# One written order for the experts' products on TensorE, and fifteen warm-up products instead of seven

## The chip, the cores and the metric

The kernel runs on one core of a Trainium2 chip. The metric is the device time of one execution in microseconds (us). The kernel before takes 1179.29 us, the median of 3 runs (1178.24 to 1180.68). Engines are named as in the profile: PE is TensorE's products, PEld its weight loads, DVE is VectorE, ACT is ScalarE, POOL is GpSimd, and SP is SyncE, which here issues most of the transfers.

## The reference: what is computed

Two layers of an encoder on 512 tokens of width 1024, all in float32. Each layer adds to `x` a mixer of two attention groups, then a cross-attention into 256 memory tokens, then a mixture of 16 experts; a last RMS norm follows. The change lies in the mixture:

```python
def expert_choice_moe(h, w_router, w_gate, w_up, w_down):
    cap = EC_CAPACITY_FACTOR * S // N_EXPERTS            # 64 tokens per expert
    affinity = jax.nn.softmax((h @ w_router).astype(jnp.float32), axis=-1)
    gate, idx = lax.top_k(jnp.swapaxes(affinity, 1, 2), cap)
    x_in = jax.vmap(lambda hb, ib: hb[ib])(h, idx)
    a = jnp.einsum('becd,edf->becf', x_in, w_gate)       # 1024 -> 512, per expert
    u = jnp.einsum('becd,edf->becf', x_in, w_up)
    y = jnp.einsum('becf,efd->becd', jax.nn.silu(a) * u, w_down)   # 512 -> 1024
    y = y * gate[..., None].astype(y.dtype)
    return jax.vmap(lambda ib, yb: jnp.zeros((S, D), yb.dtype).at[ib.reshape(-1)].add(yb.reshape(-1, D)))(idx, y)
```

## The kernel before

The two layers are written out one after the other (`for l in range(L)`). A layer's first part, the mixer and the memory attention, is not touched by the change. Then the router's affinities give each expert its 64 tokens: eight rounds of max, index and replace on DVE, two small products that place the indices (`placed`, L1012), and copies of them to `row`, `tok` and `gate` (L1014 to L1016). In layer 1 a helper `warm` (L980) puts products on PE whose result nobody reads: two behind each round, and `WARM_F` = 7 behind the index products (L1181), while the first tokens are gathered.

**Experts in pairs.** The 16 experts of a layer run as 8 pairs, p = 0 to 7. A pair's 128 tokens fill the 128 partitions: expert i of the pair has the 64 rows i\*64 to i\*64+63. For a pair the kernel does this:

- `fetch` (L1103, POOL) gathers the pair's 128 rows of 1024 values from HBM.
- `features_of(e, n)` (L1087) transposes one half of them on PE, four 128x128 transposes, and ACT (for the first pair DVE too) scales them into `xg`.
- `up_half(e, acc, w, kc)` (L1112) is half of the gate product (w = 0, into the bank `ag`) or of the up product (w = 1, into `au`): 8 products of 64 output rows by 512 columns, whose two experts alternate, i = 0, 1, 0, 1, and write different halves of the bank's partitions. In the trace each of these float32 products is two records.
- ACT takes the silu of `ag`, DVE multiplies it by `au` and the gate (L1214); `hid_t` (L1118) transposes the result and ACT copies it to `hT`.
- `down(e, n)` (L1131) is one half of the down product, 8 products of the same kind; ACT and DVE split the result into two parts `y` whose sum it is (L113, L114).
- `scatter(e, n)` (L1145) adds `y` to the tokens: for each of four blocks of 128 tokens two products, one per part, with a 0/1 matrix `sel` into a fresh bank, and DVE adds the bank to `x` (L1146). One such product is one record.

The pairs overlap by one: in pair p's turn PE does the first half of its gate product, the transposes of pair p-1's hidden values, half the features of p+1, the second gate half, pair p-1's down products, the first up half, the other features, pair p-1's two scatters, and the second up half.

**Weights.** The experts' weights are read from HBM in pieces of 512 KB ("loads" here), 24 per pair and 192 per layer, each holding two 512-column operands. SP issues them in the order of their use into some 40 slots, so that a load can start once the load 40 places before it has been used for the last time. Each load also waits for the load eight places before it, because the transfers of SP and ACT take eight completion semaphores (DMAHW0 to DMAHW7) in turn.

**What sets the order on an engine.** The kernel is written for a scheduler that puts instructions in an order of its own by its estimates of when they are ready; on the chip each engine then runs its instructions strictly in that order. `tc.issue_after(ins)` keeps what is written in its block behind `ins` on that engine. Before the change only a few such orders are given, none of them on the products of the experts, so the scheduler may put scatters between the products of an up half.

After the last pair's turn the rest is written out: `hid_t`, the second scatter of pair 6, `down(e, 0)`, the first half of `down(e, 1)`, `scatter(e, 0)`, the rest of `down(e, 1)`, `scatter(e, 1)`. In layer 1 `lnf`, the last norm's gains, is loaded by ACT (L1224) into a buffer that the gathered rows of pair 6 leave, and the final norm and four output transfers follow.

Of the kernel before, what the change touches and what calls it, by code (L numbers as in the profile page):

```python
# [16 lines left out]
P = 128  # L17
# [14 lines left out]
AFTER = 11  # L32
WARM_FROM = (8, 0)
WARM = 2
WARM_F = 7
XA = (2, 4)
MT = 6
MEM_EARLY = [0, 0, 2, 2]
# [20 lines left out]
def kernel(ctx: ExitStack, tc: tile.TileContext, a: dict, out: bass.AP):  # L59
    nc = tc.nc  # L60
# [17 lines left out]
    ident = const.tile([P, P], F32, name="ident")  # L78
# [126 lines left out]
    for l in range(L):  # L205
# [608 lines left out]
        for i in range(4):  # L814
            wh, wl = W.get()
            for h in range(4):
                for j in range(2):
                    k = 2 * i + j
# [258 lines left out]
        for p, e in enumerate(prs):  # L1077
            e.p = p

        def features_of(e, n):  # L1080

            if n == 0:
                e.xg = mp.tile([P, ND, P], F32, tag="xg", name=nm("xg"), bufs=3)
            pt = bank()
            for i in range(4):
                d = n * 4 + i
                nc.tensor.transpose(pt[:, i * P:(i + 1) * P], e.rows[:, d * P:(d + 1) * P], ident)  # L1087
            for i in range(4):
                d = n * 4 + i
                if e.p == 0 and i % 2:  # L1090
                    nc.vector.tensor_scalar(e.xg[:, d, :], pt[:, i * P:(i + 1) * P], gain(l, G_FFN, d), None, op0=ALU.mult)
                else:
                    nc.scalar.activation(e.xg[:, d, :], pt[:, i * P:(i + 1) * P], AF.Copy, scale=gain(l, G_FFN, d))  # L1093
# [12 lines left out]
        def up_half(e, acc, w, kc):  # L1106
            for j in range(4):
                k = kc * 4 + j
                if j % 2 == 0:
                    ch = [chunk(2 * e.p + i, w * 4 + k // 2) for i in range(2)]  # L1110
                for i in range(2):
                    nc.tensor.matmul(acc[i * 64:i * 64 + 64, :], e.xg[:, k, i * 64:i * 64 + 64],  # L1112
                                     ch[i][j % 2], start=k == 0, stop=k == 7)

        def hid_t(e):
            pH = bank()
            for f in range(4):
                nc.tensor.transpose(pH[:, f * P:(f + 1) * P], e.hid[:, f * P:(f + 1) * P], ident)  # L1118
            e.y = []
            e.hT = mp.tile([P, 4, P], F32, tag="sg", name=nm("hT"), bufs=1)  # L1120
            nc.scalar.copy(e.hT, pH.rearrange("p (f s) -> p f s", f=4))  # L1121

        def down(e, n, parts=(0, 1)):
            if parts[0] == 0:
                e.py = bank()
            for c in parts:
                ch = [chunk(2 * e.p + i, 8 + 2 * n + c) for i in range(2)]
                for j in range(2):
                    f = 2 * c + j
                    for i in range(2):  # L1130
                        nc.tensor.matmul(e.py[i * 64:i * 64 + 64, :], e.hT[:, f, i * 64:i * 64 + 64], ch[i][j],  # L1131
                                         start=f == 0, stop=f == 3)
            if parts[-1] == 1:
                t = mp.tile([P, 2, 512], F32R, tag="y", name=nm("y"), bufs=2)
                e.last = split(t[:, 0, :], t[:, 1, :], e.py)
                e.y.append((t[:, 0, :], t[:, 1, :]))

        def scatter(e, n):
            last = l == L - 1 and e.p == NE // 2 - 1
            for b in range(NB):  # L1140
# [1 line left out]
                o = bank()  # L1142
                sl = e.sel[:, b * P:(b + 1) * P]
                for i in range(2):
                    nc.tensor.matmul(o, sl, e.y[n][i], start=i == 0, stop=i == 1)  # L1145
                nc.vector.tensor_tensor(out=x[:, b, ns], in0=o, in1=x[:, b, ns], op=ALU.add)  # L1146
                if last and n == 0:
                    if b == 0:
# [37 lines left out]
        for e in prs:  # L1186
# [13 lines left out]
            if not end:  # L1200
                features_of(prs[e.p + 1], 1)
                if e.p + 2 < NE // 2:
                    fetch(prs[e.p + 2])
            if prev is not None and not end:
                for n in range(2):
                    scatter(prev, n)
            if not end:
                selection(e)
            up_half(e, au, 1, 1)
            if end:  # L1210
                scatter(prev, 0)
            sg = mp.tile([P, FF], F32, tag="sg", name=nm("sg"), bufs=1)
# [98 lines left out]
```

## Time and profile before

| | |
|---|---|
| median of 3 runs | 1179.29 us |
| the profiled execution | 1181.12 us |
| its span, first to last instruction | 1179.3 us |
| PE, busy and share of the span | 1141.4 us, 97% |
| DVE, ACT, POOL busy | 598.4, 489.2, 201.0 us |
| loads of the experts' weights | 384 of 512 KB |
| the experts of layer 0, first transpose to last scatter | 371.5 to 604.4 us |
| the experts of layer 1 | 937.1 to 1168.4 us |

The profiled execution is 1.8 us above the median; 1.8 us of its time lie outside its span. The span's times are counted from the first instruction. A busy PE is not PE at its peak: a row's records overlap, and what a stretch costs is read from the starts of the rows. "PEclk" is the granted share of TensorE's clock of 2.4 GHz. The DMA share is that of the core's 16 transfer engines; one at work all the time shows as 1.03 here.

### The profile page before, as it was taken

What the parts mean: (1) busy time and instruction counts of PE and PEld (TensorE: products, weight loads), DVE (VectorE), ACT (ScalarE), POOL (GpSimd) and SP (SyncE); (2) the same over time, 40 slices, a digit from 0 to 9 for tenths busy, and PEclk for the clock granted to TensorE, in tenths of its full rate; (3) what the DMA queues carried; (4) which work ended last, traced back from release to release, by engine and by line L of the source; (5) the groups of instructions that cost most, each with busy time, mean ns of one, the idle gap of its engine ahead of it and who ended that gap; (6) DMA issues with size and microseconds to landing.
All of it is one profiled execution on the core that took longest, in us unless ns stands there. A gap on an engine that the chain in (4) does not pass through costs nothing.

```text
span 1179.3 us, 16319 instructions
## 1 busy us (share of the span) xinstructions
PE 1141.4 (97%) x5842; PEld 721.4 (61%) x5842; DVE 598.4 (51%) x1354; ACT 489.2 (41%) x1116; POOL 201.0 (17%) x250
## 2 busy tenths in 40 slices
PE   7999999999999999999999999999999899999995
PEld 7977777788674343333369777777877433433332
DVE  4888967554652132222167888774565402322224
ACT  5378857464642111111043697573454221111103
POOL 2633323100011000000026323231000200000002
PEclk9999999999999999999999999999999799999998
DMA  6410111277168999999924200013833799997993
GB/s 196 134 63 10 36 37 36 72 279 293 54 231 329 411 410 410 410 409 409 358 73 134 85 1 21 16 55 114 308 114 110 300 386 410 409 411 295 410 409 156
DMA packets 78625, 259.67 MB, mean 220 GB/s; under 512 B 8528, under 2 KB 18640, under 8 KB 78544
## 3 DMA queue, kind: packets, MB, share of 16 engines
q1 hardware_dynamic: 74528, 245.41, 54.7%
q0 software_dynamic: 3584, 12.58, 2.8%
q8 instruction: 46, 0.75, 0.3%
q10 hardware_dynamic: 432, 0.63, 0.2%
q14 instruction: 35, 0.29, 0.1%
HBM read 252.30 MB, written 6.29 MB: 219 GB/s over the span
## 4 chain that ended last, share of the span: by engine, by line
PE 87%; DVE 5%; ACT 3%; issue 2%; DMA 2%; POOL 0%; SPq 0%; POOLq 0%; DVEq 0%; ACTq 0%
PE ps L1112 19%; PE ps L144 11%; PE ps L145 10%; PE ps L146 10%; PE ps L1131 10%; PE ps L1145 6%; PE ps L407 5%; PE ps L393 4%; PE ps L488 2%; DVE smm L181 2%; PE ps L1087 1%; DMA xrows<-xn 1%; PE ps L846 1%; PE ps L805 1%; PE ps L858 1%
## 5 line engine op out<-in xcount | busy, mean ns | idle before, releaser
L1112 PE MATMUL ps<-ew,xg 128*64 128x512 f32 x1024 | 260.5, 602 | 0.2 <-ACT xg L1093 0.2
L1112 PEld LDWEIGHTS ps<-ew,xg 128*64 128x64 f32 x1024 | 75.0, 137 | 142.4 <-issue 131.1
L114 DVE TENSOR_TENSOR y<-ps,y 128x512 fp32r<-128x512 f32 x32 | 21.9, 690 | 204.3 <-ACT y L113 204.3
L1131 PE MATMUL ps<-ew,hT 128*64 128x512 f32 x512 | 117.0, 593 | 0.0
L1146 DVE TENSOR_TENSOR x<-ps,x 128x512 f32<-128x512 f32 x128 | 81.0, 683 | 57.0 <-PE ps L1145 56.9
L181 DVE TENSOR_REDUCE smm<-ps 128x1 f32<-128x512 f32 (+1 forms) x144 | 97.5, 681 | 18.4 <-PE ps L488 7.7
L114 DVE TENSOR_TENSOR wlo<-raw,whi 128x1024 fp32r<-128x1024 f32 (+2 forms) x68 | 77.5, 1142 | 50.4 <-ACT whi L113 48.5
L187 ACT ACTIVATE P<-ps,smm 128x512 f32<-128x512 f32 x128 | 88.7, 696 | 27.7 <-DVE smm L181 22.0
L196 POOL TENSOR_TENSOR P<-P,smr 128x512 f32<-128x512 f32 x64 | 70.3, 1099 | 155.9 <-DVE smr L194 125.4
L113 ACT CAST whi<-raw 128x1024 fp32r<-128x1024 f32 (+2 forms) x68 | 65.8, 969 | 61.4 <-PE ps L145 32.4
L1131 PEld LDWEIGHTS ps<-ew,hT 128*64 128x64 f32 x512 | 37.3, 137 | 73.0 <-issue 72.2
L1121 ACT COPY hT<-ps 128x512 f32<-128x512 f32 x16 | 9.4, 586 | 173.9 <-PE ps L1118 173.9
L113 ACT CAST y<-ps 128x512 fp32r<-128x512 f32 x32 | 18.5, 586 | 147.9 <-PE ps L1131 139.0
L393 PE MATMUL ps<-ident,P 128*128 128x128 f32 x512 | 76.9, 274 | 2.8 <-POOL P L196 0.9
L393 PEld LDWEIGHTS ps<-ident,P 128*128 128x128 f32 x512 | 62.6, 141 | 22.8 <-issue 4.1
L1145 PE MATMUL ps<-y,sel 128*128 128x512 f32 x256 | 71.8, 412 | 2.1 <-ACT y L113 2.1
L144 PE MATMUL ps<-whi,hTh 128*128 128x384 f32 (+2 forms) x208 | 72.8, 350 | 0.3 <-ACT whi L113 0.3
L145 PE MATMUL ps<-whi,hTl 128*128 128x384 f32 (+2 forms) x208 | 72.2, 347 | 0.0
L146 PE MATMUL ps<-wlo,hTh 128*128 128x384 f32 (+2 forms) x208 | 72.1, 348 | 0.0
L1145 PEld LDWEIGHTS ps<-y,sel 128*128 128x128 f32 x256 | 44.5, 188 | 38.4 <-issue 17.8
L396 ACT COPY PT<-ps 128x512 f32<-128x512 f32 x96 | 55.9, 588 | 26.0 <-PE ps L393 25.7
L1103 POOL DMA_INDIRECT rows<-xrows,row x16 | 15.2, 953 | 245.2 <-PE ps L1145 152.6
(227 smaller groups left out, 2101.4 us busy)
## 6 DMA issues: line engine op xcount, KB each, us to landing
ew<-moe SPq DMA_DIRECT2D x384, 512.0 KB, 10.2
raw<-w_o SPq DMA_DIRECT2D x16, 512.0 KB, 3.7
raw<-w_mem_q SPq DMA_DIRECT2D x8, 512.0 KB, 4.6
raw<-w_mem_o SPq DMA_DIRECT2D x8, 512.0 KB, 3.9
xrows<-xn POOLq DMA_DIRECT2D x16, 256.0 KB, 7.5
raw<-w_in_c SPq DMA_DIRECT2D x8, 416.0 KB, 3.6
raw<-w_in_a SPq DMA_DIRECT2D x8, 384.0 KB, 5.8
raw<-w_in_b SPq DMA_DIRECT2D x8, 384.0 KB, 3.5
```

What stands on the lines that cost most here:

```text
L113: i = nc.scalar.copy(dst_hi, src)
L114: nc.vector.tensor_tensor(out=dst_lo, in0=src, in1=dst_hi.bitcast(F32), op=ALU.subtract)
L144: nc.tensor.matmul(o, lh, rh, start=start, stop=False)
L145: nc.tensor.matmul(o, ll, rh, start=False, stop=False)
L146: nc.tensor.matmul(o, lh, rl, start=False, stop=stop)
L181: nc.vector.tensor_reduce(out=m, in_=s.rearrange("p (g n) -> p g n", g=groups), axis=AX.X, op=ALU.max, negate=True)
L187: nc.scalar.activation(p[:, g * n:(g + 1) * n], s[:, g * n:(g + 1) * n], AF.Exp, bias=m[:, g:g + 1], scale=1.0 if scale is None else scale ...
L393: nc.tensor.transpose(pt[:, tb * P:(tb + 1) * P], u.p[:, tb * P:(tb + 1) * P], ident)
L1112: nc.tensor.matmul(acc[i * 64:i * 64 + 64, :], e.xg[:, k, i * 64:i * 64 + 64], ch[i][j % 2], start=k == 0, stop=k == 7)
L1131: nc.tensor.matmul(e.py[i * 64:i * 64 + 64, :], e.hT[:, f, i * 64:i * 64 + 64], ch[i][j], start=f == 0, stop=f == 3)
L1145: nc.tensor.matmul(o, sl, e.y[n][i], start=i == 0, stop=i == 1)
L1146: nc.vector.tensor_tensor(out=x[:, b, ns], in0=o, in1=x[:, b, ns], op=ALU.add)
```

## The change

All products, transposes and scatters of the experts go through one chain: each is issued behind the one before it in the order in which the kernel is written, beginning behind `placed`. Pair 0's scatters, which come in the turn of pair 1, are written behind pair 1's second up half instead of ahead of it. `WARM_F` goes from 7 to 15.

```diff
-WARM_F = 7
+WARM_F = 15
...
+        turn = [placed]
+
+        def in_turn(*args, **kw):
+
+            with tc.issue_after(turn[0].ins):
+                turn[0] = nc.tensor.matmul(*args, **kw)
+
         def features_of(e, n):
...
-                nc.tensor.transpose(pt[:, i * P:(i + 1) * P], e.rows[:, d * P:(d + 1) * P], ident)
+                with tc.issue_after(turn[0].ins):
+                    turn[0] = nc.tensor.transpose(pt[:, i * P:(i + 1) * P], e.rows[:, d * P:(d + 1) * P], ident)
...
-                    nc.tensor.matmul(acc[i * 64:i * 64 + 64, :], e.xg[:, k, i * 64:i * 64 + 64],
-                                     ch[i][j % 2], start=k == 0, stop=k == 7)
+                    in_turn(acc[i * 64:i * 64 + 64, :], e.xg[:, k, i * 64:i * 64 + 64],
+                            ch[i][j % 2], start=k == 0, stop=k == 7)
...
-                    nc.tensor.matmul(o, sl, e.y[n][i], start=i == 0, stop=i == 1)
+                    in_turn(o, sl, e.y[n][i], start=i == 0, stop=i == 1)
...
-            if prev is not None and not end:
+
+            if prev is not None and not end and e.p > 1:
                 for n in range(2):
                     scatter(prev, n)
             if not end:
                 selection(e)
             up_half(e, au, 1, 1)
+            if e.p == 1:
+                for n in range(2):
+                    scatter(prev, n)
```

The transposes of `hid_t` and the products of `down` are changed in the same way. How the built programs differ is shown below at three places; numbers behind a name are buffers.

**PE, layer 1, the turn of pair 5**, from the first up half to the second: L1112 (now L1085) is `up_half`, L1087 (now L1095) `features_of`, L1145 (now L1085 as well, since the helper issues it) `scatter` of pair 4. Before:

```order
L1112 MATMUL ps_9858<-ew_9859,xg_9621 64x512
L1087 MATMUL ps_9875<-ident,rows_9713 128x128 x4
L1145 MATMUL ps_9886<-y_9835,sel_9747 128x512 x2
L1112 MATMUL ps_9858<-ew_9861,xg_9621 64x512
L1112 MATMUL ps_9858<-ew_9859,xg_9621 64x512
L1112 MATMUL ps_9858<-ew_9861,xg_9621 64x512
L1145 MATMUL ps_9890<-y_9835,sel_9747 128x512 x2
L1145 MATMUL ps_9894<-y_9835,sel_9747 128x512
L1112 MATMUL ps_9858<-ew_9867,xg_9621 64x512
L1145 MATMUL ps_9894<-y_9835,sel_9747 128x512
```

and with the change:

```order
L1085 MATMUL ps_9866<-ew_9875,xg_9629 64x512
L1085 MATMUL ps_9866<-ew_9877,xg_9629 64x512
L1085 MATMUL ps_9866<-ew_9875,xg_9629 64x512
L1085 MATMUL ps_9866<-ew_9877,xg_9629 64x512
L1095 MATMUL ps_9883<-ident,rows_9721 128x128 x4
L1085 MATMUL ps_9894<-y_9843,sel_9755 128x512 x2
L1085 MATMUL ps_9898<-y_9843,sel_9755 128x512 x2
L1085 MATMUL ps_9902<-y_9843,sel_9755 128x512 x2
```

Before, the first up half's eight products stand in runs of one, three, one and three, with scatter products between; now they stand in one run, and the sixteen scatter products in another. Before, the turns of pairs 3 to 7 in layer 0 and of pairs 4 to 7 in layer 1 have such a place, and in layer 0's turn of pair 1 the scatters split an up half into runs of five and three; now no turn has one, and those of pairs 2 to 6 have the form shown second.

**SP, layer 1, the loads around the last norm's gains**, with the semaphores that each waits for. Before:

```order
L1054 DMA ew_9869<-moe 128x1024 [waits DMAHW3_49,PE_49]
L1054 DMA ew_9920<-moe 128x1024 [waits DMAHW5_49,PE_49]
L1054 DMA ew_9922<-moe 128x1024 [waits DMAHW6_49,PE_49]
L1054 DMA ew_9928<-moe 128x1024 [waits DMAHW7_49,PE_49]
...
L1054 DMA ew_9948<-moe 128x1024 [waits DMAHW3_49,PE_49]
L1054 DMA ew_9950<-moe 128x1024 [waits DMAHW4_49,PE_49]
```

and with the change:

```order
L1054 DMA ew_9928<-moe 128x1024 [waits DMAHW4_49,PE_49]
L1054 DMA ew_9930<-moe 128x1024 [waits DMAHW5_49,PE_49]
L1054 DMA ew_9936<-moe 128x1024 [waits DMAHW6_49,PE_49]
L1054 DMA ew_9938<-moe 128x1024 [waits DMAHW0_49,PE_49]
...
L1054 DMA ew_9983<-moe 128x1024 [waits DMAHW6_49,PE_49]
L1054 DMA ew_9989<-moe 128x1024 [waits DMAHW7_49,PE_49]
```

The semaphore that SP's loads leave out there belongs to the load of `lnf` that ACT issues (in both programs ACT's load stands behind the first scaling of pair 6's second features). Before it is DMAHW4, and the load into `ew_9950` is the first that waits for it; now it is DMAHW7, and three more loads stand ahead of the first that waits, the one into `ew_9989`.

**ACT, the first work of layer 1's mixer**: L150 is a sum of squares, L116 the first part of a transposed block of `x`, L113 the first part of a weight. Before:

```order
L116 ACTIVATE hTh_5403<-ps_5412,gains 128x512
L150 ACTIVATE junk_5524,nss_5467<-x 128x512
L116 ACTIVATE hTh_5419<-ps_5421,gains 128x512
L113 CAST whi_5392<-raw_5391 128x2x384
L116 ACTIVATE hTh_5419<-ps_5428,gains 128x512
L113 CAST whi_5398<-raw_5397 128x2x384
```

and with the change:

```order
L116 ACTIVATE hTh_5403<-ps_5412,gains 128x512
L116 ACTIVATE hTh_5419<-ps_5421,gains 128x512
L116 ACTIVATE hTh_5419<-ps_5428,gains 128x512
L116 ACTIVATE hTh_5435<-ps_5437,gains 128x512
L113 CAST whi_5392<-raw_5391 128x2x384
L113 CAST whi_5398<-raw_5397 128x2x384
```

The first weight's cast, for which the first product of the layer waits, stands behind two more activations and ahead of one sum of squares that it followed before.

## Rows read from the trace of the kernel before

**Rows 1.** The page's part 1: busy us, share of the span and instructions of each engine.

```profile
PE 1141.4 (97%) x5842; PEld 721.4 (61%) x5842; DVE 598.4 (51%) x1354; ACT 489.2 (41%) x1116; POOL 201.0 (17%) x250
```

**Rows 2.** Windows: stretch, us, busy us (x instructions) by engine, PEclk, DMA share, GB/s.

```profile
471.62:501.86 30.24, 30.16 (x124) 11.11 (x125) 7.68 (x12) 4.54 (x12) 0.94 (x1) 1.00 1.03 410
1013.16:1039.34 26.18, 26.18 (x127) 10.89 (x125) 7.40 (x12) 4.45 (x12) 0.94 (x1) 1.00 1.03 410
1065.85:1096.09 30.24, 30.16 (x124) 11.12 (x125) 7.68 (x12) 4.53 (x12) 0.00 (x0) 1.00 0.78 298
```

**Rows 3.** PE in order of time (start, us, records at x): turn of pair 3, then 5.

```profile
1028.48 3.91 PE L1145 MATMUL ps<-y,sel 128*128 128x512 f32 x16
1032.32 7.09 PE L1112 MATMUL ps<-ew,xg 128*64 128x512 f32 x32
...
1082.96 1.93 PE L1112 MATMUL ps<-ew,xg 128*64 128x512 f32 x6
```

**Rows 4.** SP's loads for pair 7's up product: layer 0, then layer 1.

```profile
L1054 SPq DMA_DIRECT2D ew<-moe x8: 327/327/328, 557.1 to 566.1; - x8
...
DMA to landing us min/median/max: 10.2/10.2/10.2
...
L1054 SPq DMA_DIRECT2D ew<-moe x8: 328/328/328, 1128.5 to 1137.4; - x8
...
DMA to landing us min/median/max: 10.2/10.2/10.5
```

**Rows 5.** PE and DVE in order of time: layer 0 from pair 7's up product on, then layer 1.

```profile
576.27 0.59 PE L1112 MATMUL ps<-ew,xg 128*64 128x512 f32 x1
...
582.10 5.36 PE L1112 MATMUL ps<-ew,xg 128*64 128x512 f32 x22
...
599.56 1.94 PE L1131 MATMUL ps<-ew,hT 128*64 128x512 f32 x8
...
602.21 0.69 DVE L114 TENSOR_TENSOR y<-ps,y 128x512 fp32r<-128x512 f32 x1 [1.73 <-ACT y L113]
...
1140.25 0.59 PE L1112 MATMUL ps<-ew,xg 128*64 128x512 f32 x1
...
1146.09 5.36 PE L1112 MATMUL ps<-ew,xg 128*64 128x512 f32 x22
```

**Rows 6.** ACT in order of time, first work of layer 1.

```profile
606.17 0.63 ACT L150 ACTIVATE junk<-x 128x512 bf16<-128x512 f32 x1
...
606.78 0.68 ACT L116 ACTIVATE hTh<-ps,gains 128x512 fp32r<-128x512 f32 x1
```

**Rows 7.** PE in order of time: the first pair of layer 0, then of layer 1.

```profile
371.51 1.04 PE L1087 MATMUL ps<-ident,rows 128*128 128x128 f32 x8
372.74 3.65 PE L1112 MATMUL ps<-ew,xg 128*64 128x512 f32 x16 [0.20 <-ACT xg L1093]
...
929.59 3.29 PE L984 MATMUL ps<-x 128*128 128x256 f32 x14
937.14 1.97 PE L1087 MATMUL ps<-ident,rows 128*128 128x128 f32 x8 [4.26 <-DMA rows<-xrows,row]
939.04 5.56 PE L1112 MATMUL ps<-ew,xg 128*64 128x512 f32 x16
```

**Rows 8.** SP's loads' waits (us, times, longest); the issue of `lnf`, its landing.

```profile
SPq L1054 <- PE ps L1112: 38.8, 33, 22.7
...
SPq L1054 <- DMA lnf<-lnf: 14.8, 1, 14.8
...
L1224 ACTq DMA_DIRECT2D lnf<-lnf x1: 334/334/334, 1082.8 to 1082.8; - x1
...
DMA to landing us min/median/max: 3.4/3.4/3.4
```

**Rows 9.** PE early in layer 1's mixer, and the window behind it.

```profile
669.74 1.14 PE L488 MATMUL ps<-kk,qs 128*128 128x512 f32 x2 [1.29 <-DVE qs L114]
...
670.00:673.30 3.30, 3.30 (x14) 2.04 (x15) 3.21 (x14) 3.07 (x6) 1.31 (x2) 0.50 0.00 0
```

More of the change, by code (lines that the diff above doesn't have):

```diff
@@ L1117, in hid_t @@
             for f in range(4):
-                nc.tensor.transpose(pH[:, f * P:(f + 1) * P], e.hid[:, f * P:(f + 1) * P], ident)
+                with tc.issue_after(turn[0].ins):
+                    turn[0] = nc.tensor.transpose(pH[:, f * P:(f + 1) * P], e.hid[:, f * P:(f + 1) * P], ident)
             e.y = []
@@ L1130, in down @@
                     for i in range(2):
-                        nc.tensor.matmul(e.py[i * 64:i * 64 + 64, :], e.hT[:, f, i * 64:i * 64 + 64], ch[i][j],
-                                         start=f == 0, stop=f == 3)
+                        in_turn(e.py[i * 64:i * 64 + 64, :], e.hT[:, f, i * 64:i * 64 + 64], ch[i][j],
+                                start=f == 0, stop=f == 3)
             if parts[-1] == 1:
```

## The prediction

> **What bounds the kernel now.** I read the page's part 1 first: PE is busy for 97% of the span, every other engine for 61% or less [rows 1]. Next come windows of one turn each, where the reader should compare the length with the DMA column [rows 2]. A turn of layer 1 whose products stand unbroken takes 26.18 us, a turn with scatters between the products of an up half 30.24 us, at the same granted clock, 1.00, and with the same products. PE in order of time shows why [rows 3]: an unbroken up half costs 7.09 / 32 = 0.22 us a record, while a run of three products (six records) costs 1.93 us where 1.33 would be due; each break leaves a half-bank product without its partner and costs about half a us. A broken turn loses 4.06 us to that.
>
> The transfers are the second bound, and a near one. In layer 0's broken turn they run at 410 GB/s with a share of 1.03, so they are never idle. SP issues eight loads in 9.0 us, one per 1.28 us, and each lands 10.2 us later, so eight are in flight [rows 4]. A turn's 24 loads need 30.7 us: PE at 30.24 us a turn already eats slowly into the lead of the loads, and at 26.18 us would run into them. That lead is the number on which this prediction rests. In layer 0 the first load of pair 7's up product lands at 557.1 + 10.2 = 567.3 and is first used at 576.27: 8.9 us. In layer 1 it lands at 1128.5 + 10.2 = 1138.7 and is used at 1140.25: 1.5 us [rows 4, 5]. Layer 1 has less because its stream starts late and is stopped once; both are seen in SP's waits, below.
>
> **The change, part by part.** *Breaks on PE.* The order rows show no break left. Layer 0 has three full pieces of 4.06 us (12.2), some 3.4 in the half turn ahead of them and 4.2 in the last turn, estimates by the same half us a break: 19.8 us of PE time. Layer 1 has two full pieces: 8.1 + 3.4 + 4.2 = 15.7. If PE alone set the end, that would be the gain. But PE then arrives at weights that have not landed, so I work out each layer's end from its last up load instead.
>
> *Layer 0.* Transfers are saturated, so PE's new order cannot bring the loads forward: the last up load of pair 7 still lands at 566.1 + 10.2 = 576.3. Six records that need it follow (1.35 us), so the up product ends at 577.65; in the kernel before it ended at 582.10 + 5.36 = 587.46 [rows 5]. That is 9.8 us earlier. Behind it stand, before and now, the last transposes, scatters and the down product. By PE's prices this tail is now 1.95 (eight scatters) + 0.5 (transposes) + 1.95 + 5.3 (24 down records) + 1.95 + 1.76 = 13.4 us, to 591.06. The tail before took 14.04 us, to 599.56 + 1.94 = 601.50. So the down product ends 10.4 us earlier. Its weights land behind the up loads, eight more at 1.28 us: 586.5, ahead of their last use at 589.3, so they do not bind.
>
> Two small terms go against it. The last scatter takes the two parts of `y` alternately now, and the second part is ready only behind DVE's 0.69 us [rows 5], where four first parts filled that time: +0.65. At the start of layer 1 the first weight's cast, for which PE waits, stands behind two more activations of 0.68 us and ahead of one sum of squares of 0.63 that it followed [rows 6]: +0.6, to nothing at best and 1.3 at worst; I take the difference. Layer 0: -10.4 + 0.65 + 0.6 = **-9.2 us**. Pair 0's scatters move behind the other up half of pair 1; they are the same products, and a delay there (about 0.65 us of PE) is hidden by the later wait for loads.
>
> *Layer 1, warm-ups.* Seven products took 3.29 us in 14 records and PE then idled 4.26 us until the rows landed. The first pair's transposes cost 1.97 us where layer 0's cost 1.04, and its first product 5.56 instead of 3.65 [rows 7]: half clock. Fifteen products are 30 records, 7.05 us at that price, and end at 936.6, 0.5 us ahead of the landing at 937.14, so they delay nothing by themselves, and the first block becomes 0.93 + 1.91 less 0.2 = 2.6 us shorter. If the clock stays low anyway this is 0; if the products overrun, they cost at most a us. Since the loads there wait for slots that PE frees (the longest wait is 22.7 us [rows 8]), the stream shifts with PE: I take -2.3.
>
> *Layer 1, the stop at `lnf`.* One load of SP waited 14.8 us for the load of `lnf`, issued by ACT at 1082.8 and landed 3.4 us later, at 1086.2 [rows 8]. The turn around it ran at 298 GB/s instead of 410: 30.24 x (1 - 298 / 410) = 8.3 us of stream lost, so a stop costs its length less 6.5 us, what was in flight. Now PE reaches the place that lets ACT issue `lnf` 6.0 us earlier (2.6 from the warm clock, 3.4 from the breaks ahead of it), so it lands at 1080.2; and three more loads go out first (the order rows: `ew_9989` instead of `ew_9950`), so the stop begins 3.8 us later in the stream, less the stream's own shift of 2.3. The stop shrinks to 14.8 - 6.0 - 1.5 = 7.3 us or a little more and costs about 1.1 us: -7.2. Bounds: whole stop left, 0; none left, -8.3.
>
> So layer 1's last up load lands 2.3 + 7.2 = 9.5 us earlier: 1137.4 + 10.5 - 9.5 = 1138.4. The up product ends at 1139.75 instead of 1146.09 + 5.36 = 1151.45 [rows 4, 5], 11.7 earlier; the same shorter tail gives 0.65, and the last scatter's first block is ready for DVE 0.25 earlier: **-12.5 us**, below what PE could gain by itself there (15.7 + 2.6 = 18.3).
>
> **Sum.** -9.2 - 12.5 = -21.7: the profiled execution's 1181.12 becomes 1159.4; it stood 1.8 above the median, so I predict **1158 us**. Less than 2.4 us (0.2%) could not be told from no change by a measurement of this kernel; faster means under 1176.9.
>
> **The rivals.** *The clock falls in the load-paced stretch (slower).* PE would work 1.76 us (eight records) and wait 0.8 in every 2.56 us (two loads) over pair 6's second half turn, pair 7 and the tail, some 46 us of PE work a layer. A gap of 1.29 us early in layer 1's mixer is followed by a window at a granted 0.50 [rows 9], 1.2 GHz, and at that level the transposes cost 1.9 times as much [rows 7]. If all of the stretch ran so, each layer would take 41 us more, of which up to 9.4 fill waits: +32 a layer, about 1222 us. Against it: one gap, and one wait of 4.26 us, stand behind those falls, with other engines' chains in between; here PE keeps two thirds. It is slower than before only if about half of the stretch is at half clock: 0.04. Milder swings or a stop at `lnf` left whole cost 7 to 18 us and end at 1165 to 1176, part of it inside my range; above it: 0.07.
>
> The Trainium skill, "TensorE: Matmul & The Clock Gate", section "A second HAM failure mode: psum-queue depth-cycling", tells of a kernel whose many micro-idles between groups of products made the clock swing between its two levels, at a loss of throughput. By that rule this change, which swaps slow but steady products for quick ones with waits, gives back its gain, and the sum would be the 1222 us above, or part of the way there. The trace of the kernel before shows such a fall in one place and none in the broken turns.
>
> *The loads do not bind.* If SP's loads ran on earlier than I think, PE's own time would decide: -19.8 - 18.3 = -38, about 1143 us. The share of 1.03 through layer 0 speaks against it: 0.04.
>
> *Nothing changes.* If the breaks only filled time that PE would have spent waiting for loads, the end stays near 1179. Layer 1's lead of 1.5 us speaks for it, layer 0's 8.9 us against; it also needs the stop to stay whole: 0.05. That the change does not do what it says is ruled out by the order rows.
>
> **How the numbers follow.** Forecast 0.80, clock or stop in a milder form 0.07, loads not binding 0.04, no change 0.05, clock falls for good 0.04. Faster: 0.80 + 0.07 + 0.04 = 0.91; same 0.05; slower 0.04. The range takes the bounds of the unknown prices: low, the stop gone (-1.1), the cast free (-0.6) and the down weights alone at the end of each layer (-2.4 a layer, what PE's tail exceeds them), 1151; high, the stop whole (+7.2) and the clock giving back about 1.4 a layer, 1168.
>
> **What the next profile would show.** Turns of pairs 2 to 5 at 26.2 us in both layers, with runs of 16 and 32 records at 0.22 us; PE's waits on landed weights, almost none before, at 7 to 9 us a layer in the turns of pairs 6 and 7; the transfers at 410 GB/s to the end; layer 0's experts ending at about 594 instead of 604.4; SP's wait on `lnf` near 7 us instead of 14.8; a granted clock of 1.00 at 937 and the first product at 3.65 us. Wrong would be: a clock below 1.00 in the last turns (first rival), an up product of pair 7 that ends well before 577.65 (loads not binding), or a stop at `lnf` as long as before.

## The result and the profile after

The changed kernel takes **1161.89 us**, the median of 4 runs (1161.59 to 1162.22), against 1179.21 us of the kernel before beside it: a ratio of 0.9853, 95% interval 0.9839 to 0.9866. That is 17.3 us faster; 1158 us was forecast, within 1151 to 1168. The profiled execution took 1162.13 us, its span is 1160.3 us. Run again later beside other kernels, it took 1162.75 us, ratio 0.9855 (0.9832 to 0.9878).

Part 1 of the page of the changed kernel, which answers to [rows 1]:

```profile
PE 1118.9 (96%) x5858; PEld 721.5 (62%) x5858; DVE 596.1 (51%) x1354; ACT 489.1 (42%) x1116; POOL 200.9 (17%) x250
```

PE's share fell by one per cent only: a row of PE reaches to its modelled end, so a wait of 0.8 us between two groups of products shows as 0.2 us of idleness. The waits are better read from the length of a turn. Windows of the changed kernel, in the columns of [rows 2]: three turns of layer 0 (from one pair's second features to the next pair's; the third ends with pair 7's up product), then the same three of layer 1:

```profile
484.12:510.30 26.18, 26.18 (x127) 10.93 (x125) 7.40 (x12) 4.44 (x12) 0.94 (x1) 1.00 1.03 409
510.30:540.66 30.36, 29.53 (x126) 11.49 (x124) 7.41 (x12) 4.44 (x12) 0.00 (x0) 1.00 1.03 409
540.66:576.47 35.81, 34.38 (x138) 12.65 (x137) 7.41 (x12) 3.40 (x8) 0.00 (x0) 1.00 1.03 409
...
1042.26:1068.43 26.17, 26.17 (x126) 10.89 (x124) 7.41 (x12) 4.44 (x12) 0.94 (x1) 1.00 1.03 410
1068.43:1097.08 28.65, 28.24 (x127) 11.42 (x125) 7.41 (x12) 4.44 (x12) 0.00 (x0) 1.00 0.91 355
1097.08:1133.05 35.97, 34.50 (x138) 12.60 (x137) 7.41 (x12) 3.40 (x8) 0.00 (x0) 1.00 1.03 409
```

Unbroken turns take 26.18 us now in both layers, until PE reaches weights that have not landed: in the turns that end at 540.66 and at 1097.08 and in those behind them PE waits for landings. The granted clock is 1.00 in all six windows. One window has transfers below their rate (355 GB/s): the stop at `lnf`, which is still there.

PE in order of time in the changed kernel: the end of layer 0's experts, the first work of layer 1, then the first and last products of layer 1's experts (L1085 issues all three kinds of product; the tiles tell them apart):

```profile
370.33 1.04 PE L1095 MATMUL ps<-ident,rows 128*128 128x128 f32 x8
...
559.25 2.36 PE L1085 MATMUL ps<-ew,hT 128*64 128x512 f32 x8 [0.21 <-DMA ew<-moe]
...
572.05 2.35 PE L1085 MATMUL ps<-ew,xg 128*64 128x512 f32 x8 [0.20 <-DMA ew<-moe]
574.61 1.93 PE L1085 MATMUL ps<-ew,xg 128*64 128x512 f32 x6 [0.21 <-DMA ew<-moe]
576.47 2.12 PE L1085 MATMUL ps<-y,sel 128*128 128x512 f32 x8
...
588.15 1.94 PE L1085 MATMUL ps<-ew,hT 128*64 128x512 f32 x8
590.83 0.49 PE L1085 MATMUL ps<-y,sel 128*128 128x512 f32 x1 [0.74 <-ACT y L113]
591.55 1.89 PE L1085 MATMUL ps<-y,sel 128*128 128x512 f32 x7 [0.23 <-DVE y L114]
...
597.86 0.44 PE L144 MATMUL ps<-whi,hTh 128*128 128x384 f32 x1 [0.93 <-ACT whi L113]
...
918.52 6.74 PE L984 MATMUL ps<-x 128*128 128x256 f32 x30
927.20 1.09 PE L1095 MATMUL ps<-ident,rows 128*128 128x128 f32 x8 [1.94 <-DMA rows<-xrows,row]
928.32 3.65 PE L1085 MATMUL ps<-ew,xg 128*64 128x512 f32 x16
931.90 0.66 PE L1095 MATMUL ps<-ident,rows 128*128 128x128 f32 x4
...
1131.19 1.93 PE L1085 MATMUL ps<-ew,xg 128*64 128x512 f32 x6 [0.22 <-DMA ew<-moe]
...
1144.74 1.94 PE L1085 MATMUL ps<-ew,hT 128*64 128x512 f32 x8
```

Groups of eight records start 2.56 us apart there (572.05, 574.61): two loads, as forecast. The warm-ups end before the rows land, and the first 16 records take 3.65 us. Two rows of the kernel before that were not shown, for the same places:

```profile
608.24 0.44 PE L144 MATMUL ps<-whi,hTh 128*128 128x384 f32 x1 [0.34 <-ACT whi L113]
...
1163.56 1.94 PE L1131 MATMUL ps<-ew,hT 128*64 128x512 f32 x8
```

With [rows 5, 7] the span divides so (us; the end of a row is its start and its length):

| from the end of the line above to | before | after | difference | forecast |
|---|---|---|---|---|
| first transpose of layer 0's experts | 371.51 | 370.33 | -1.18 | 0 |
| end of its last down product | 229.99 | 219.76 | -10.23 | -10.4 |
| first product of layer 1 | 6.74 | 7.77 | +1.03 | +1.25 |
| first transpose of layer 1's experts | 328.90 | 329.34 | +0.44 | 0 |
| end of its last down product | 228.36 | 219.48 | **-8.88** | -12.3 |
| end of the span | 13.80 | 13.62 | -0.18 | -0.25 |

The first line is not the change's: up to there the work is the same, and over the executions profiled here that place came between 369.25 and 372.45.

### The profile page after: what moved, and what is told of

It reads as the page before. It is cut to its first block, busy times and chain, and to the rows that moved or that the text cites. A ratio compares the mean times of both kernels' runs of the same rounds, so it can differ in the third digit from the quotient of the medians.

```text
span 1160.3 us, 16352 instructions
## 1 busy us (share of the span) xinstructions
PE 1118.9 (96%) x5858; PEld 721.5 (62%) x5858; DVE 596.1 (51%) x1354; ACT 489.1 (42%) x1116; POOL 200.9 (17%) x250
## 4 chain that ended last, share of the span: by engine, by line
PE 75%; DMA 15%; DVE 5%; ACT 3%; issue 1%; POOL 1%; SPq 0%; DVEq 0%; ACTq 0%; POOLq 0%
PE ps L1085 24%; DMA ew<-moe 12%; PE ps L144 11%; PE ps L145 10%; PE ps L146 10%; PE ps L407 5%; PE ps L393 4%; DVE smm L181 2%; PE ps L488 1%; DMA xrows<-xn 1%; PE ps L846 1%; PE ps L805 1%; PE ps L858 1%; PE ps L1095 1%; PE ps L250 1%
## 5 line engine op out<-in xcount | busy, mean ns | idle before, releaser
L1085 PE MATMUL ps<-ew,xg 128*64 128x512 f32 x1024 | 239.5, 597 | 2.7 <-DMA ew<-moe 2.5
L1085 PEld LDWEIGHTS ps<-ew,xg 128*64 128x64 f32 x1024 | 71.8, 136 | 144.2 <-issue 119.8
L1085 PE MATMUL ps<-ew,hT 128*64 128x512 f32 x512 | 121.0, 596 | 1.7 <-DMA ew<-moe 1.7
L1155 DVE TENSOR_TENSOR x<-ps,x 128x512 f32<-128x512 f32 x128 | 78.3, 684 | 37.7 <-PE ps L1085 37.7
L113 ACT CAST whi<-raw 128x1024 fp32r<-128x1024 f32 (+2 forms) x68 | 65.6, 969 | 61.7 <-PE ps L145 32.8
L1085 PEld LDWEIGHTS ps<-ew,hT 128*64 128x64 f32 x512 | 38.3, 137 | 80.0 <-issue 65.4
L113 ACT CAST y<-ps 128x512 fp32r<-128x512 f32 x32 | 18.5, 586 | 138.8 <-PE ps L1085 138.8
L1085 PE MATMUL ps<-y,sel 128*128 128x512 f32 x256 | 64.6, 400 | 3.0 <-ACT y L113 2.1
L1101 ACT ACTIVATE xg<-ps,gains 128x128 f32<-128x128 f32 x120 | 34.7, 371 | 62.0 <-PE ps L1095 61.7
L1085 PEld LDWEIGHTS ps<-y,sel 128*128 128x128 f32 x256 | 46.5, 188 | 19.6 <-ACT y L113 5.6
```

Source lines behind the costliest of these rows:

```text
L113: i = nc.scalar.copy(dst_hi, src)
L1085: turn[0] = nc.tensor.matmul(*args, **kw)
```

## The experiments

Ratios are to the kernel before in the same job, with 95% intervals.

**1. The written order alone**

```diff
-WARM_F = 15
+WARM_F = 7
```

> The changed kernel with 7 warm-up products in layer 1 as before, not 15: the written order alone. My theory: the first block of layer 1's experts runs at half clock again, 2.6 us longer (the first product of 16 records at 5.6 us instead of 3.65), the slots come free 2.3 us later, so the loads and the end move by 2.3 to 2.7 us: 1164.4 us. Rival (the loads bind, so the warm-ups are hidden): 1161.9 us, the same as the changed kernel.

1163.14 us, ratio 0.9867 (0.9852 to 0.9882).

**2. The warm-ups alone**, in the kernel before

```diff
-WARM_F = 7
+WARM_F = 15
```

> The kernel before with 15 warm-up products in layer 1 instead of 7: the warm-ups alone. My theory: the clock stands at 1.00 when the first tokens land, the first block is 2.6 us shorter, PE sets the end of layer 1: 1179.2 - 2.6 = 1176.6 us. Rival (warm-ups hidden behind loads): 1179.2 us.

1177.0 us, ratio 0.9984 (0.9975 to 0.9993): 1.6 us less by medians, 1.9 by the ratio, where 2.6 was expected. In run 1 the missing warm-ups cost 1.3 us by medians and 1.7 by the ratios, but its interval overlaps the changed kernel's. The order is worth the rest: 15.4 us in run 1, far outside the noise. PE in order of time at the first pair of layer 1, the order alone:

```profile
927.30 1.80 PE L1095 MATMUL ps<-ident,rows 128*128 128x128 f32 x8 [4.88 <-DMA rows<-xrows,row]
...
933.54 0.66 PE L1095 MATMUL ps<-ident,rows 128*128 128x128 f32 x4
```

The block takes 4.70 us with fifteen warm-ups in the changed kernel (927.20 to 931.90), and 4.64 to 4.70 in every other profile with fifteen but that of run 10, which has other products there. With seven it took 7.39 us in [rows 7] (to 944.53), 6.24 here, where the clock came back earlier (the granted clock of 927 to 933 is 0.72; of 937 to 943 in the kernel before 0.51), and 4.70 in run 8. What seven warm-ups lose differs between executions; the forecast took one profile's loss for the rule.

Run 2 is not the warm-ups alone, though: the scheduler also wrote one turn of layer 1, that of pair 4, in another order. Four products stand ahead of its second features with fifteen warm-ups:

```profile
1047.79 1.89 PE L1112 MATMUL ps<-ew,xg 128*64 128x512 f32 x8
```

and one in the kernel before:

```profile
1050.71 1.02 PE L1112 MATMUL ps<-ew,xg 128*64 128x512 f32 x2
```

That turn, from one transpose of hidden values to the next, takes 25.30 us (1036.41 to 1061.71) instead of 26.51 (1039.34 to 1065.85). If these 1.2 us reach the end, little of the 1.6 to 1.9 is left for the warm-ups. Whether the loads hide the warm-ups in the changed kernel (the rival of run 1) is not settled.

**3. No load of SP behind `lnf`**

```diff
-            nc.scalar.dma_start(lnf, a["lnf"])
+            nc.gpsimd.dma_start(lnf, a["lnf"])
```

> The changed kernel with the load of the last norm's gains issued by POOL instead of ACT, so that no load of SP waits for it. My theory: the stop of 9.7 us (3.8 us of stream by the window of pair 5's turn) is gone, the last up load of layer 1 lands 3.2 to 3.8 us earlier and the end with it: 1158.4 us. Rival (PE waits only where loads are late for other reasons, or PE's order binds behind the stop): under 1 us gained, 1161 or more.

1157.61 us, ratio 0.9826 (0.9813 to 0.9839): 0.0027 below the changed kernel's, 3.2 us (4.3 by medians), where 3.5 was expected. The stop was still on the path in the changed kernel. The last load-paced group of the up product starts 199.07 us after the first transpose of layer 1's experts here (1126.56 less 927.49), 203.99 in the changed kernel.

**4. The features ahead of the up half**

```diff
             au = bank()
-            up_half(e, au, 1, 0)
             if not end:
                 features_of(prs[e.p + 1], 1)
...
+            up_half(e, au, 1, 0)
```

> The changed kernel with the second features of the next pair ahead of the first up half instead of behind it. ACT issues the load of the last norm's gains behind the first scaling of these features, so my theory (the place of the features on PE sets when that load goes out) expects its issue 3.5 us earlier, about 141 - 3.5 = 138.7 us after the first transpose of layer 1's experts instead of 142.2. The semaphore it takes moves too: the first load that waits for it is the one into ew_9956, four loads ahead of ew_9989, so the stop begins 4 x 1.28 = 5.1 us earlier. Stop: 9.7 + 5.1 - 3.5 = 11.3 us, cost 11.3 - 6.5 = 4.8 instead of 3.2: 1.6 us slower than the changed kernel, 1163.5 us. Rival (the stop is a fixed matter of the load's own landing): 9.7 us and the same time.

1165.09 us, ratio 0.988 (0.9859 to 0.99), beside the changed kernel at 1162.75: 2.3 us slower, where 1.6 was expected and the rival said none. The two intervals overlap, so the time does not decide; the trace does. What SP's loads waited for, and the issue of `lnf`, in the changed kernel:

```profile
SPq L1054 <- DMA lnf<-lnf: 9.7, 1, 9.7
...
L1237 ACTq DMA_DIRECT2D lnf<-lnf x1: 334/334/334, 1069.3 to 1069.3; - x1
```

and with the features first:

```profile
SPq L1054 <- DMA lnf<-lnf: 12.3, 1, 12.3
...
L1237 ACTq DMA_DIRECT2D lnf<-lnf x1: 335/335/335, 1069.4 to 1069.4; - x1
```

The first transpose of layer 1's experts is at 929.74 us in this run, so `lnf` goes out 139.7 us behind it, against 142.1 in the changed kernel: earlier by 2.4 us, not by 3.5. The place of the features on PE does set the issue. The missing 1.1 us were spent in the turns: features that stand alone between two halves are one more change to full-width products and back, and each of the three turns ahead takes 26.51 us (1041.97 to 1068.48 is the last) instead of 26.18. The stop begins four loads earlier all the same, and is 2.6 us longer, near the 2.3 us of the time.

**5. Odd breaks put back, and 6. even breaks.** In the turns of pairs 2 to 6, `up_half` calls `scatter` for one block behind the products named, the fourth block behind the half:

```diff
+            cut = [[(c, n, [b]) for b, c in enumerate((1, 4, 5))] for n in range(2)]
...
-            up_half(e, au, 1, 0)
+            up_half(e, au, 1, 0, cut[0])
```

> The changed kernel with the sixteen scatter products of the turns of pairs 2 to 6 put back between the products of the two up halves, behind products 1, 4 and 5 of each (runs of 1, 3, 1, 3). The partner theory (a run of an odd number of half-bank products leaves one without its partner): eight odd runs a turn at half a us, PE-bound turns of about 30.2 us, and about 1183 us. The switch theory (any change between the two kinds of product costs): the same, 30.2 us.

For the even breaks `(2, 4, 6)` stands in place of `(1, 4, 5)`.

> The same as the odd breaks, and as many, but behind products 2, 4 and 6 of each up half (runs of 2, 2, 2, 2). The partner theory: no product is left alone, turns stay at 26.2 to 26.8 us and the time at 1162 to 1163 us. The switch theory: eight breaks a turn cost the same half us each, turns of about 30.2 us, about 1183 us.

Odd: 1203.21 us, ratio 1.02 (1.0182 to 1.0219). Even: 1173.28 us, ratio 0.995 (0.9933 to 0.9967). Neither theory's numbers. PE in order of time, one turn of layer 0 from features to features, odd breaks:

```profile
501.65 0.65 PE L1095 MATMUL ps<-ident,rows 128*128 128x128 f32 x4
...
502.70 1.07 PE L1085 MATMUL ps<-ew,xg 128*64 128x512 f32 x2
...
504.37 1.93 PE L1085 MATMUL ps<-ew,xg 128*64 128x512 f32 x6
...
533.70 0.66 PE L1095 MATMUL ps<-ident,rows 128*128 128x128 f32 x4
```

and even breaks:

```profile
490.51 0.65 PE L1095 MATMUL ps<-ident,rows 128*128 128x128 f32 x4
...
491.56 1.08 PE L1085 MATMUL ps<-ew,xg 128*64 128x512 f32 x4
...
519.19 0.65 PE L1095 MATMUL ps<-ident,rows 128*128 128x128 f32 x4
```

Turns take 32.05 us with odd breaks, 28.68 with even ones, 26.18 with none; PE waits for no weights in these turns. Apart from the block of the hidden transposes, both have eight blocks of full-width products (128 output rows; the experts' products have 64) where the changed kernel has one: (28.68 - 26.18) / 7 = **0.36 us a break of any kind**. Oddness adds (32.05 - 28.68) / 8 = **0.42 us a run**, the time of one product (two records) alone: a run of one takes 1.07 us like a run of two (1.08), a run of three 1.93.

The same two prices add up to what a broken turn lost before the change. In the window 1065.85 to 1096.09 of [rows 2] PE has six full-width blocks where an unbroken turn has two, and between them six runs, all odd (3, 29, 3, 1, 3 and 9 products), where an unbroken turn has none: 4 x 0.36 + 6 x 0.42 = 3.96 of the 4.06 us. Rows of that turn, beside the order rows of the change:

```profile
1066.76 1.93 PE L1112 MATMUL ps<-ew,xg 128*64 128x512 f32 x6
...
1081.90 0.66 PE L1087 MATMUL ps<-ident,rows 128*128 128x128 f32 x4
...
1091.50 4.51 PE L1112 MATMUL ps<-ew,xg 128*64 128x512 f32 x18
```

The kernels' times hold more than the turns. Even breaks make layer 0's experts only 1.7 us longer than in the changed kernel (221.47 against 219.76), since five turns of 2.5 us more mostly fill the waits for weights; in layer 1 it is 9.0 us, and there SP's stop at `lnf` grew from 9.7 to 19.3 us (31.2 with odd breaks).

The Trainium skill, "TensorEngine Tiling (Array Packing)", section "Key Properties", says that a change of the tiling mode, not just of the tile, drains the engine, and that different tiles run in parallel. Both parts agree with these rows: the 0.36 us stand at each block, that is at a change from products of 64 output rows to products of 128 and back, and the 0.42 us are a tile without company. The page gives no price for either, and that a drain is what takes the 0.36 us no run shows.

**7. Half the loads, new order**

```diff
         def load(u, slot):
 
+            if u % 2:
+                loaded[u] = whole[u - 1]
+                return
```

> The changed kernel with every second load of the experts' weights left out: both experts of a pair use the even expert's weights, so the values differ from the reference's. PE's instructions are the same, the weight traffic is half. My theory: PE alone sets the end, and the part of its gain that waits for loads took back comes out: layer 0 another 9.4 us, layer 1 another 9.4: about 1143 us, with no PE wait for weights in the turns of pairs 5 to 7. Rival (what PE waits for is not the transfers' rate): 1158 us or more.

1139.45 us, ratio 0.9672 (0.9658 to 0.9687): 0.0181 below the changed kernel's, 21.3 us (22.4 by medians), where 19 was expected. PE in order of time, the second features of the last two turns, and the end of pair 7's up product:

```profile
510.66 0.66 PE L1100 MATMUL ps<-ident,rows 128*128 128x128 f32 x4
...
536.83 0.66 PE L1100 MATMUL ps<-ident,rows 128*128 128x128 f32 x4
...
566.00 2.12 PE L1090 MATMUL ps<-y,sel 128*128 128x512 f32 x8
```

These stretches take 26.17 and 29.17 us; in the changed kernel 30.36 and 35.81. So PE waits 4.19 + 6.64 = 10.8 us for weights in layer 0, and by the same sums (28.65 and 35.97) 9.3 in layer 1. As a whole layer 0's experts become 10.8 us shorter (208.93 instead of 219.76), layer 1's 10.7 (208.76 instead of 219.48; the stop at `lnf` is gone as well). That is where the part of PE's gain went that the time does not show.

**8. Half the loads, old order**: the same edit in the kernel before.

> The kernel before with the same every second load left out (values differ from the reference's). My theory: PE sets its end already, so the loads taken away give at most the few waits seen: 1176 to 1179 us. Rival (the broken order only filled the time in which PE would have waited for loads): about 1143 us, like the changed kernel with half the loads.

1138.14 us, ratio 0.9651 (0.9634 to 0.9668): the rival's number, but not for its reason. PE in order of time, a turn of layer 0:

```profile
482.59 3.60 PE L1117 MATMUL ps<-ew,xg 128*64 128x512 f32 x16
486.12 0.66 PE L1092 MATMUL ps<-ident,rows 128*128 128x128 f32 x4
486.53 3.91 PE L1150 MATMUL ps<-y,sel 128*128 128x512 f32 x16
490.37 7.09 PE L1117 MATMUL ps<-ew,xg 128*64 128x512 f32 x32
```

From pair 2's turn on there are no breaks: with half the loads the scheduler, which orders by its estimates of readiness, wrote these turns unbroken by itself. The kernel is not the one that was meant, and whether the old breaks only filled waits it does not test; run 5 answers that on PE: there breaks lengthen turns with every weight landed ahead. In pair 1's turn a run of one product and a run of fifteen are left, and each layer's experts take 0.9 us more than in run 7, two odd runs by the price above. The run also points to where the breaks came from. The loads are all that was taken away, so the scheduler seems to have put scatters between the products because it expected weights late that were in time (8.9 us ahead in layer 0); its estimates themselves were not looked at.

**9. Scatters in the waits.** In the last turn of each layer:

```diff
-            up_half(e, au, 1, 0)
+            up_half(e, au, 1, 0, [(4, 0, [0]), (8, 0, [1])] if end else ())
...
-            up_half(e, au, 1, 1)
+            up_half(e, au, 1, 1, [(4, 0, [2, 3])] if end else ())
```

> The changed kernel, in the last turn of each layer: eight of the sixteen scatter products of pair 6 stand in pairs between groups of four products of the up product, where PE waits 0.8 us for each two loads; four more stand ahead of the last hidden transposes and four behind. My theory: the last up load lands when it did, and 8 x 0.24 us are gone from what follows it: 1.9 us a layer, 3.9 in all, 1158.0 us. Rival (the clock or a later wait, of the down product's loads or the transposes for their input, takes it back): 1161 us or more.

1160.31 us, ratio 0.9838 (0.9823 to 0.9853): 0.0015 below the changed kernel's, within the intervals. Less than half of what was expected. A pair of scatter products fits a wait of 0.8 us (0.66 us from start to start); the four ahead of the last group took 1.13 us, and that group then started without a wait, late by PE's own work.

**10. Expert by expert**

```diff
-            for j in range(4):
-                k = kc * 4 + j
...
-                for i in range(2):
...
+            for i in range(2):
+                for j in range(4):
+                    k = kc * 4 + j
                     in_turn(acc[i * 64:i * 64 + 64, :], e.xg[:, k, i * 64:i * 64 + 64],
```

> The changed kernel with the eight products of each up half in another order: the four of the first expert, then the four of the second, instead of in turns. Same products, same number, no scatter between. The partner theory (two half-bank products of the two experts run beside each other): hardly any has a partner, so a half of 16 records takes near 16 x 0.43 = 6.9 us instead of 3.6, and the kernel well over 1300 us. The switch theory (only a change to another kind of product costs): 3.6 us a half and a time near 1162 us.

1208.02 us (one run). Again neither number. PE in order of time:

```profile
479.06 8.97 PE L1085 MATMUL ps<-ew,xg 128*64 128x512 f32 x32
487.95 0.66 PE L1126 MATMUL ps<-ident,sg 128*128 128x128 f32 x4
...
492.52 0.64 PE L1085 MATMUL ps<-ew,hT 128*64 128x512 f32 x1
492.95 0.59 PE L1085 MATMUL ps<-ew,xg 128*64 128x512 f32 x1
493.00 0.59 PE L1085 MATMUL ps<-ew,hT 128*64 128x512 f32 x1
493.38 0.59 PE L1085 MATMUL ps<-ew,xg 128*64 128x512 f32 x1
```

Two halves take 8.89 us instead of 7.02, 4.4 a half: 0.9 more, not 3.3 more. The last four rows show how: records of the down product start among the last ones of the up product. A product's partner need not stand next to it; it can be one of a later group, as long as only half-width products (64 output rows) stand between. So, against what the part on the order of an engine says, products do not always start in the written order: the first one of the down product starts at 492.52, ahead of a record of the up product at 493.38. In the starts of single records each group of four products (eight records) overlaps the next by four records, 0.43 us apart, and the first four and last four records between two full-width blocks run alone: 20 steps of 0.43 for the 32 records, 8.6 of the 8.89 us. Here the reach was two products. So the partner theory needs a correction: what costs is a product without a partner within that reach, be it the odd one between two full-width blocks (run 5) or the first and the last two in this order, where the two halves are even.

**11. Three edits on top of the change.** `lnf` by POOL; in each layer's last turn

```diff
-                for n in range(2):
-                    down(prev, n)
+                down(prev, 0)
+                if end:
+                    down(prev, 1, (0,))
+                    scatter(prev, 0, [0])
+                    down(prev, 1, (1,))
...
+            up_half(e, au, 1, 0, [(4, 0, [1]), (8, 0, [2])] if end else ())
...
+            up_half(e, au, 1, 1, [(4, 0, [3])] if end else ())
```

and layer 0's last scatter with its four first parts ahead.

> The changed kernel with three edits: the last norm's gains loaded by POOL (worth 3.7 us when alone); in each layer's last turn four pairs of pair 6's scatter products stand one by one in the waits for weights (one between the last down groups, three between up groups), four products ahead of the last hidden transposes and four behind; and layer 0's very last scatter has its four first parts ahead of the four second parts. Expected: 1161.5 - 3.7 - 2 x 1.6 (scatters in waits, less a switch each) - 0.5 (last scatter) = about 1154 us. Rival (the switches cost what the waits give): 1157.5 us.

**1153.7 us**, ratio 0.9787 (0.9768 to 0.9805), beside the changed kernel at 1162.75: faster than both kernels. PE in order of time, layer 0, pair 7's up product with a pair of scatter products in each gap, then the last scatter in one piece:

```profile
568.60 0.73 PE L1085 MATMUL ps<-y,sel 128*128 128x512 f32 x2
569.26 1.97 PE L1085 MATMUL ps<-ew,xg 128*64 128x512 f32 x8
571.16 0.73 PE L1085 MATMUL ps<-y,sel 128*128 128x512 f32 x2
...
589.38 2.11 PE L1085 MATMUL ps<-y,sel 128*128 128x512 f32 x8 [0.74 <-ACT y L113]
```

The groups of eight start 2.56 us apart as they did, with the scatters in what was a wait. The three edits were not run one by one, but they lie at different places of the trace. Against the changed kernel's profile, layer 0's experts, where only the scatters in the waits count, are 1.6 us shorter; the first product of layer 1 comes 1.05 us sooner behind them (ACT's cast comes sooner as well there); layer 1's experts are 5.9 us shorter, the largest part with the stop at `lnf` (run 3: 4.9).

**12. The changed kernel beside runs 4, 10 and 11**

> The changed kernel itself, on the chip of the runs beside it: 1161.5 us within 1 us.

1162.75 us (4 runs, 1159.25 to 1163.67), where 1161.5 within 1 us was expected. In its profile the experts of both layers take 0.9 us more (220.62 and 220.34) than in the first profile of the same kernel, so a difference of that size between two single profiles says nothing.

## Why the prediction was right, and by how much it was off

**The bound changes hands: right.** Turns at 26.2 us until the loads bind, then PE in step with landings; layer 0's experts end 10.2 us earlier where 10.4 was forecast. PE's own gain there would be 9 to 11 us more, and run 7 brings it out. The price behind it, half a us for a product that a break leaves without its partner, was right in size and mixed two things: 0.36 us for any break (run 6) and 0.42 for an odd run (run 5).

**Layer 0's two counter-terms: right.** The alternating last scatter waits for DVE behind its first record: the next one starts 0.72 us later (590.83, 591.55) instead of 0.25, so 0.47 us were lost where 0.65 was written. The wait for the cast of layer 1's first weight grew from 0.34 to 0.93 us, 0.59 where 0.6 was written. Together the two cost 1.03 us where 1.25 was written.

**The clock falls (first rival): refuted.** From 559.25 to 574.61 and over the same groups in layer 1 PE waits some 0.8 us in every 2.56, and the granted clock is 1.00 in both layers. The Trainium skill, "TensorE: Matmul & The Clock Gate", section "A second HAM failure mode: psum-queue depth-cycling", tells of a kernel in which it swung; it did not here, and the measurement decides. The fall behind a gap of 1.29 us [rows 9] does not come every time: the first profile of the changed kernel has the same gap, up to 659.32, and a clock of 1.00 behind it, while that of run 12 falls to 0.50 there. Why is open. The kernel before also shows 0.50 in 915.6 to 922.4 and near it from 937 on, so the prediction's "in one place" was too few.

**Loads not binding, and no change: refuted,** by the waits above and by the interval.

**Layer 1: right in kind, 3.4 us too good,** in two terms. *The stop at `lnf`.* The step "PE reaches the place that lets ACT issue `lnf` 6.0 us earlier" failed: it was 3.6 (from 1082.8 to 1069.3, less the 9.94 us by which layer 1's experts began earlier). The old order had the features behind the first product of the up half (at 1081.90); the written order has them behind all eight (at 1068.43), which gives 2.6 us of the gain back. The order rows show both, and I used them only for the breaks. So the stop was 9.7 us, not 7.3; by "its length less 6.5" that costs 3.2 us, and the window with 355 GB/s gives 28.65 x (1 - 355 / 410) = 3.8, where 1.1 was forecast. Run 4's trace bears out the place, run 3 the sign and, with 3.2 to 4.9 us, the size. By this the last group of the up product started 203.99 us behind the first transpose, where 1138.4 less 937.14, 201.3, was due: 2.7 us late.

*The tail behind the last up load.* It was priced at 1.35 + 13.4 = 14.75 us and takes 15.5 in both layers (574.61 to 590.09, 1131.19 to 1146.68). Six records that start a run cost 1.9 us, as [rows 3] show, not 6 x 0.22, and each change between half and full width costs its part of 0.36. In layer 0 the last group started 0.5 us ahead of the forecast (574.61, where 576.3 less 1.18 was due), which by luck hid most of it. (The parts written for layer 1, 11.7, 0.65 and 0.25, also add up to 12.6, not 12.5.)

**The warm-ups: right in kind, sized by one execution.** The block did become 2.7 us shorter than in the profile before, but the times of runs 1 and 2 give 1.9 us at most, and run 2's gain is in part another order. What the warm-ups are worth by themselves stays open.

**From the profile to the median.** Profiled against profiled, 19.0 us were gained where 21.7 were forecast. The profiled execution before stood 1.8 us above its median, the one after 0.2: 1.2 us of that lay ahead of the experts of layer 0. I took the same 1.8 off for the changed kernel, whose profile stood only 0.2 above its median; this is 1.6 of the 3.9 us by which the forecast missed. The 1.2 us were luck for the comparison of the two profiles: without them it would show 17.8.

The 0.44 us by which the first transposes of layer 1's experts came later, counted from the layer's first product, lie within what this stretch varies by: in the profiles with the written order and all loads it took between 328.69 and 329.98 us.

## What to carry to other kernels

Where products on half of TensorE's columns alternate with full-width ones, let the two halves alternate, keep them even between full-width blocks and the blocks few: here an odd run cost 0.42 us, and each block 0.36. Before adding up a faster engine's gain, find the lead of each load over its use, and price the end from the last landing; then put the full-width work into the waits that remain, in pieces that fit. When an order is written out, look at what else moved: here a transpose that had gone early by accident had released a transfer on another queue.

## What the runs showed that was not expected

A product on one half of the columns finds its partner beyond its neighbours: with four products of one expert ahead of four of the other, a half takes 4.4 us, not 6.9, and records of the next group start among those of this one (run 10). A change between half and full width and back costs 0.36 us even where the halves are even (run 6). And the scheduler's order moves with edits elsewhere: with half the loads the old source gives the unbroken order almost by itself (run 8), and with more warm-ups one turn changes (run 2), so a run of one edit need not test that edit alone.
